# Another order table for the five engine queues of a hybrid decoder layer

## The chip, the cores and the metric

The kernel runs on one core of a Trainium2 chip, in one launch. The metric is the device time of an execution in microseconds (us). The engines are PE (TensorE, matrix products), DVE (VectorE), ACT (ScalarE), POOL (GpSimd) and SP (which here only issues loads). DMA transfers are issued by SP and by POOL.

## What is computed

One decoder layer on x of 512 tokens by 1024 channels, in float32. Two causal mixers run side by side on one input projection, native sparse attention (NSA) and a gated DeltaNet (GDN); a gated feed-forward network (FFN) with a short convolution follows.

```python
h = x @ w_in[l]
...
y_a = nsa_attention(nsa_q, cmp_k, cmp_v, slc_k, slc_v, win_k, win_v, nsa_gate, ...) @ w_nsa_out[l]
y_b = gated_deltanet(gdn_qkv, gdn_beta, gdn_decay, gdn_gate, ...) @ w_gdn_out[l]
mix = (jax.nn.sigmoid(gate_a) * y_a + jax.nn.sigmoid(gate_b) * y_b) @ w_o[l]
x = layer_norm(DEEPNORM_ALPHA * x + mix, ln1_g[l], ln1_b[l])
f = conv_ffn(x, ffn_w_up[l], ffn_conv_w[l], ffn_w_down[l])
x = layer_norm(DEEPNORM_ALPHA * x + f, ln2_g[l], ln2_b[l])
...
def conv_ffn(x, w_up, conv_w, w_down):
    h = causal_dwconv(x @ w_up, conv_w)
    gate, val = jnp.split(h, 2, axis=-1)
    return (jax.nn.silu(gate) * val) @ w_down
```

## The kernel before

Every float32 product is made of three products of rounded parts: a weight block `raw` is loaded (SP), ACT writes its high part `wh` (L481, L1504, L1562), DVE or POOL the rest `wl = raw - wh` (L485, L1505, L1563), and PE multiplies high by high, low by high and high by low. The activations exist as such pairs too (`xh`, `xl`; `mh`, `ml`).

**Stages by time.** Up to about 360 us the kernel does the input projection (`gps`, L495 to L498), the GDN chunks and the NSA heads, interleaved. To 400 us follows the merge, then the output projection and the first norm; from some 480 us FFN-up, from about 705 us FFN-down, at the end the second norm.

**Attention.** For each head and block PE makes scores (`aps`), DVE finds the row minimum (L1072), ACT takes exponentials (L1074), and L1085 scales the probabilities `sc` by the reciprocal sum and the gate, on DVE for most blocks and on POOL for some. PE then transposes `sc` (L1101). The GDN part around it keeps POOL busy: L551 is a power for a norm (`rn0`, `rn1`, `so`) over sums `ss` (L704, from ACT's L703), L485 a `wl`, L746 and L747 masks times decays (`grh`, `grl`), L769 a mask on `at`, L754 a product `db`.

**FFN-up.** 22 groups p of 128 gate and 128 value channels. An ordinary group (`plain`) makes `pu0` (gate) and `pu1` (value) by L1568. Seven groups (`seven`) are made by seven half-size products instead of eight, by L1515, in the PSUM tiles `px`, `pz`, from a combination of weight blocks and of activations (`sh0` to `sh3`, `sl0` to `sl3`, made in `x_sums`); ACT and DVE put the results together in `wf0` and `wf1` (L1524, L1529, L1534, L1537, L1539). A product into `px` cannot begin until the partial sum in it has been copied to `wf`. The combined weights `usum` are built in device memory by POOL's accumulating DMAs; those for FFN-down are `wsum` (L539), those of the output projection `osum`. Each group then passes three taps of the convolution (`fa0`, `fa1`: ACT L1545, twice DVE L1548), a gate `fth` (ACT L1606, DVE L1607, POOL L1608) and is written out as parts for FFN-down (`ph`, `pl`, `sr0` to `sr3`: L1612 to L1623, tiles `pha`, `pla`, `sr0a` and so on).

**Order.** The program is written stage by stage, and a table `QUEUES` then sets the order of every engine's instructions: for each engine the list of its instructions' numbers in the program, in the order in which they are to be issued. `queues` (L348) walks through it and makes every instruction follow the one before it in the list. Each engine works its list strictly in order; an instruction that waits holds up all behind it on that engine. Dependences between engines (data, and buffers to become free) are semaphores, and do not depend on the table. Buffers go round in small sets (`raw`, `wh`, `wl` three each, `raw7` one), so that a load for a later group is issued when the last reader of an earlier one is done.

Of the kernel before, what the change touches and what calls it, by code (L numbers as in the profile page):

```python
# [70 lines left out]
def layout(a):  # L71
# [67 lines left out]
    "PE": """0-9 11-12 10 13-32 41 38 35-37 33 42-43 53 39 34 54 44-45 47-48 40 50-51 46 52 49 56 59 62 57 55 58 65-66 60 63-64 61  # L139
74 68 67 77 71 78 72-73 75-76 86 79 69 87-89 83 70 80 84 81 98 82 99 92-93 85 107 90 108-109 94 110 91 95 111-112 96  # L140
100 113 97 114-115 101-102 116-123 103 124-148 155-178 104 149-151 105 152-153 106 154 183-204 207 205 208 206 209-229
179-182 235 230 236-251 259 252 260 253 261-264 254 265 255 266-267 231-232 256-257 302-303 258 268 233 269-270 304
234 305-307 271-282 308 310-311 360 309 283-298 361-363 312 364-367 313 368 314 369-371 388 315 372 389-390 373-376
391-392 377 393 378 394 379-382 395 383 299-300 396-399 444-445 301 446-450 400-401 416 402-406 417 407-411 418-433
456 434-439 457-459 451 316-317 320 318 321-323 319 460-463 324-327 464-466 328 332-339 329-331 467-472 513 340-347
473-475 348-355 452 476-477 501 356-359 384-387 478-479 514-519 412-415 502-503 520-521 504 522-525 440 453 441 454
442 455 443 526-531 723-725 532 480-484 505 507-508 726-729 533 730 506 485 731 534-536 486-487 509-510 541 732 542
488-489 733-734 490 751-752 735-736 491-492 543 753 737 754-755 493 544 511 494 512 738 495 546-547 739 496 545 497
740 756-757 548 498-499 549 758-760 500 550-551 761 560-561 762 741 763-764 742-744 562 565 552 745 566 746 563-564
537 591 765 592 766 538-540 567 767 581-582 768 553-554 593 568 594-597 569 555 570 598-600 556-557 583 558 585 584  # L150
# [12 lines left out]
1222-1223 1216 1121 1224 924-931 1122 1217 932-935 1225 1123 1233-1234 1124-1125 960 1126-1128 961 1129-1130 962-963
1131-1133 1218 1134-1136 964 1226 965 1235-1236 1227-1228 966 1141-1143 1238 1144-1145 967-968 1239 1146-1149 969 1237
970 1240 1150-1152 971-972 1153-1154 1252 1179 1241 973 1242 1253 1155 1180 974 1181-1182 975 1243 1254-1256 976
1156-1157 1183-1184 1158 1257 1159 1185 1160-1161 1186 1258 1244 1162 1187 1163-1164 1188-1190 1245 1191-1193 1246
1025-1026 1137-1139 1259 1140 1260-1261 1027 1262 1028 1273 1247 1194 1274 1195 1283 1196-1197 1248-1249 1198-1199
1284 1250 1200 1285 1251 1201 1263 1202 1165 1275 1169 1286-1287 1277 1307 1288 1278 1264 1170 1308-1310 1289-1290
1311 1166 1279 1167 1171 1280 1172-1173 1168 1174 1276 1403-1404 1312-1317 1175 1405 1176-1178 1265 1281 1406 1282
1407 1318 1266-1267 1319 1408 1320 1268 1291 1269 1409 1292 1270-1272 1321-1327 1229 1328-1329 1293-1294 1231 1410  # L170
1422-1423 1330 1295 1230 1296 1411 1424-1425 1412 1426 1413 1427 1297-1299 1232 1300-1303 1414 1428 1304 1379 1305
1415 1380 1416-1417 1306 1418 1429-1432 1443-1444 1381-1386 1419-1421 1387-1389 1433-1434 1445 1447-1448 1435 1390
1436 1391 1437 1331 1449 1332 1446 1453 1438-1439 1450-1452 1440 1454 1392 1477 1393-1394 1441 1395-1397 1455 1458
1478 1459 1479 1442 1480 1398 1460 1456-1457 1461-1462 1333 1463 1399 1481 1400-1401 1482-1483 1472-1473 1484-1485
# [1592 lines left out]
```

## Time and profile before

| | us |
|---|---|
| median of 3 runs | 837.82 (837.53 to 840.38) |
| profiled execution | 837.5 |
| its span in the trace | 835.7 |
| PE busy | 806.7 |
| DVE busy | 641.3 |
| ACT busy | 432.1 |
| POOL busy | 195.2 |

The profiled execution lies 0.3 us under the median, and 1.8 us of it lie around the span. Its mean granted clock on TensorE is 0.992. In a group's row of the profile stand line, engine, operation, tiles and shapes; "<-" in brackets names what ended the idle time ahead of it. Line numbers are those of the kernel before. In the new kernel the table is one text line shorter, so that line numbers behind it are one lower there (L1085 becomes L1084).

### The profile page before, as it was taken

To read this page: it belongs to the slowest core of one execution; us is meant where nothing else is said; L and a number is where in the kernel's file an instruction comes from. 1 tells how busy PE (TensorE), PEld (TensorE's weight loads), DVE (VectorE), ACT (ScalarE), POOL (GpSimd) and SP (SyncE) were. 2 spreads that over 40 slices of the span, in tenths; PEclk is the share of its full clock that TensorE was granted. 3 is DMA by queue.
4 is the path that set the end of the run, shared out by engine and by line. 5 is a ranking of instruction groups with operands and counts; after the bars stand their busy time and mean duration, and the time that the engine had idled before them with its cause. 6 is when DMAs were issued, how large, how long until landed. Compare 5 with 4: busy or idle time off the path is not lost.

```text
span 835.7 us, 12479 instructions
## 1 busy us (share of the span) xinstructions
PE 806.7 (97%) x4390; PEld 681.9 (82%) x4390; DVE 641.3 (77%) x1391; ACT 432.1 (52%) x965; POOL 195.2 (23%) x186
## 2 busy tenths in 40 slices
PE   9999999999999999999899999989999999999996
PEld 8788888778788888888787898968788888888875
DVE  5668689889678965565479879857777887788788
ACT  4463686774576764332344235543645654565541
POOL 0334825042275211332100112220011121100001
PEclk9999999999999999999999999999999999999999
DMA  8326129078246936446566697789483468475674
GB/s 277 95 86 214 30 76 249 26 192 186 56 131 156 187 90 153 151 127 153 213 252 203 239 185 234 182 220 201 137 276 114 140 156 197 138 206 173 205 238 148
DMA packets 53406, 139.80 MB, mean 167 GB/s; under 512 B 3936, under 2 KB 5088, under 8 KB 53088
## 3 DMA queue, kind: packets, MB, share of 16 engines
q1 hardware_dynamic: 36064, 92.88, 34.8%
q0 software_dynamic: 17280, 46.14, 24.2%
q8 instruction: 34, 0.56, 0.3%
q14 instruction: 28, 0.23, 0.1%
HBM read 136.91 MB, written 48.23 MB: 222 GB/s over the span
## 4 chain that ended last, share of the span: by engine, by line
PE 77%; DVE 10%; DMA 7%; ACT 3%; issue 2%; POOL 0%; SPq 0%; DVEq 0%; ACTq 0%; POOLq 0%
PE pu L1568 15%; PE gps L495 8%; PE gps L497 8%; PE gps L498 8%; PE px L1645 4%; PE px L1515 4%; PE pz L1645 4%; PE pz L1515 3%; DMA raw<-in_up 2%; PE pout L1115 2%; PE aps L1101 2%; DMA raw<-usum 2%; PE pu L1645 2%; PE pm L495 2%; PE pm L497 2%
## 5 line engine op out<-in xcount | busy, mean ns | idle before, releaser
L495 PE MATMUL gps<-xh,wh 128*128 128x512 f32 x320 | 125.2, 402 | 3.1 <-ACT mt L1147 2.3
L498 PE MATMUL gps<-xh,wl 128*128 128x512 f32 x320 | 125.7, 400 | 0.0
L497 PE MATMUL gps<-xl,wh 128*128 128x512 f32 x320 | 125.1, 399 | 0.0
L1568 PE MATMUL pu<-mh,wh 128*128 128x512 f32 x208 | 80.4, 398 | 2.2 <-ACT wh L1562 2.2
L1568 PE MATMUL pu<-mh,wl 128*128 128x512 f32 x208 | 79.7, 399 | 1.0 <-DVE wl L1563 1.0
L1568 PE MATMUL pu<-ml,wh 128*128 128x512 f32 x208 | 79.8, 396 | 0.0
L1608 POOL TENSOR_TENSOR fth<-fth,fa 128x512 f32<-128x512 f32 x22 | 32.4, 1474 | 197.3 <-DVE fth L1607 150.6
L495 PEld LDWEIGHTS gps<-xh,wh 128*128 128x128 f32 x320 | 60.5, 190 | 15.1 <-issue 3.3
L485 DVE TENSOR_TENSOR wl<-raw,wh 128x512 fp32r<-128x512 f32 x66 | 48.4, 738 | 29.7 <-PE gps L498 13.6
L498 PEld LDWEIGHTS gps<-xh,wl 128*128 128x128 f32 x320 | 60.5, 190 | 11.5 <-POOL wl L485 0.6
L497 PEld LDWEIGHTS gps<-xl,wh 128*128 128x128 f32 x320 | 60.5, 190 | 10.4
L1470 ACT ACTIVATE wh<-raw 128x512 fp32r<-128x512 f32 x67 | 39.9, 626 | 38.9 <-PE px L1645 9.5
L1562 ACT ACTIVATE wh<-raw 128x512 fp32r<-128x512 f32 x52 | 32.6, 628 | 51.5 <-PE pu L1568 41.5
L1471 DVE TENSOR_TENSOR wl<-raw,wh 128x512 fp32r<-128x512 f32 x67 | 44.4, 691 | 16.7 <-ACT wh L1470 16.6
L1563 DVE TENSOR_TENSOR wl<-raw,wh 128x512 fp32r<-128x512 f32 x52 | 38.2, 739 | 21.3 <-ACT wh L1562 18.1
L1504 ACT ACTIVATE wh<-raw 128x512 fp32r<-128x512 f32 x49 | 30.6, 628 | 40.2 <-PE px L1515 15.2
L1548 DVE SCALAR_TENSOR_TENSOR fa<-pu,fcw,fa 128x511 f32<-128x511 f32 (+1 forms) x60 | 44.3, 745 | 7.7 <-ACT fa L1545 7.4
L481 ACT ACTIVATE wh<-raw 128x512 fp32r<-128x512 f32 x46 | 28.8, 627 | 38.4 <-PE gps L497 29.6
L1568 PEld LDWEIGHTS pu<-mh,wh 128*128 128x128 f32 x208 | 39.7, 191 | 8.8 <-ACT wh L1562 2.6
L1568 PEld LDWEIGHTS pu<-mh,wl 128*128 128x128 f32 x208 | 39.6, 191 | 8.8 <-DVE wl L1563 2.6
L485 POOL TENSOR_TENSOR wl<-raw,wh 128x512 fp32r<-128x512 f32 x30 | 41.8, 1413 | 19.9 <-PE gps L498 5.4
L1568 PEld LDWEIGHTS pu<-ml,wh 128*128 128x128 f32 x208 | 39.6, 190 | 6.2
(498 smaller groups left out, 2252.8 us busy)
## 6 DMA issues: line engine op xcount, KB each, us to landing
raw<-in_wT SPq DMA_DIRECT2D x40, 512.0 KB, 3.7
raw<-in_up SPq DMA_DIRECT2D x37, 512.0 KB, 4.6
wsum<-in_down POOLq DMA_DIRECT2D x6, 2816.0 KB, 21.7
usum<-in_up POOLq DMA_DIRECT2D x6, 1792.0 KB, 15.8
raw<-wsum SPq DMA_DIRECT2D x20, 512.0 KB, 3.6
raw<-in_down SPq DMA_DIRECT2D x15, 512.0 KB, 4.3
osum<-in_wo POOLq DMA_DIRECT2D x6, 1024.0 KB, 10.8
wsum<-wsum POOLq DMA_DIRECT2D x2, 2816.0 KB, 15.0
```

The lines of the kernel that those rows point to most:

```text
L485: eng.tensor_tensor(wl, r, wh.bitcast(F32), op=OP.subtract)
L495: i = PE.matmul(ps, wh[k], mh_(k), start=(k == 0), stop=False)
L497: PE.matmul(ps, wh[k], ml_(k), start=False, stop=False)
L498: PE.matmul(ps, wl[k], mh_(k), start=False, stop=(k == n - 1))
L1470: A.activation(hi, raw[:, i], AF.Copy)
L1471: V.tensor_tensor(lo, raw[:, i], hi.bitcast(F32), op=OP.subtract)
L1515: stop=k == 3 and w is lo) if False else PE.matmul(
L1548: V.scalar_tensor_tensor(acc[:, n:], ps[:, :S - n], w[:, i:i + 1], acc[:, n:], op0=OP.mult, op1=OP.add)
L1562: A.activation(hi, r, AF.Copy)
L1563: V.tensor_tensor(lo, r, hi.bitcast(F32), op=OP.subtract)
L1568: q = PE.matmul(ps, w[:, j], x[:, k, :], start=k == 0 and i == 0, stop=k == KD - 1 and i == 2, skip_group_check=True)
L1645: m = PE.matmul(ps, a[x](j)[:, ts], w[y], start=first and i == 0, stop=last and i == 2, skip_group_check=True)
```

## The change

Only the numbers in `QUEUES` change. Every instruction, its engine and its buffers stay as they are; each of the five engines gets them in another order, of which long stretches are the old one (between 180 and 361 us of the profile nothing moves).

```diff
-    "Pool": """2 1 0 8 10 9 12 3 11 13 4 15 5-7 16-17 19 113 20-22 27-28 14 33 25 23 34 29 39 30-32 18 43 40 44 24 41 115 26 54 45 35
-55-36 105 48 42 38 62 37 112 49 51 47 52 64-66 68 107 67 69 57 46 58 50 116 104 92 56 117 59 61 53 63 86 80 87 108 60
...
+    "Pool": """2 1 0 8-9 3 10-13 4 15 5-7 16-17 19 18 20-22 27 14 28 33 25 23 34 29 39 30 105 31-32 40 43 38 37 44 24 41 112 54 35 45
+55 48 36 113 42 49 51 47 52 26 115 107 64-69 50 46 57 62 58 116 104 92 56 117 59 61 53 63 86 80 87 108 60 75 90 76-78
```

Three places show it, in the rows of the queues (line, operation, tiles with their numbers, shape).

**First place, near 168 to 175 us of the profile.** POOL, before and then after (`at`, `grh`, `grl`, `xs` belong to the GDN chunks; `rn0_1930` needs `ss_1929`):

```order
L485 TENSOR_TENSOR wl_2420<-raw_2416,wh_2418 128x512
L485 TENSOR_TENSOR wl_2424<-raw_2416,wh_2422 128x512
L746 TENSOR_TENSOR grh_2134<-cst_321,gdh_340 128x512
L769 TENSOR_TENSOR at_1559<-at_1559,cst_321 128x512
L747 TENSOR_TENSOR grl_2135<-cst_321,gdl_341 128x512
L551 TENSOR_TENSOR rn0_1930<-ss_1929,minus_half_333 128x4
```

```order
L484 TENSOR_TENSOR wl_2420<-raw_2416,wh_2418 128x512
L482 CAST wh_2422<-raw_2416 128x512
L484 TENSOR_TENSOR wl_2424<-raw_2416,wh_2422 128x512
L550 TENSOR_TENSOR rn0_1930<-ss_1929,minus_half_333 128x4
L768 TENSOR_TENSOR at_1559<-at_1559,cst_321 128x512
L745 TENSOR_TENSOR grh_2134<-cst_321,gdh_340 128x512
L793 COPY xs_2188<-cst_321 128x64
L746 TENSOR_TENSOR grl_2135<-cst_321,gdl_341 128x512
```

DVE at the same place, before and then after:

```order
L1105 TENSOR_TENSOR ptl_347<-aps_2270,pth_346 128x2x128
L1076 RECIPROCAL mn_2277<-mn_2277 128x1
L1085 TENSOR_SCALAR sc_2276<-sc_2276,mn_2277,gsig_110 128x384
L1072 ISA sc_2670,mn_2671<-aps_2669,cst_321 128x512
L1072 ISA mn_2671 128x1
L485 TENSOR_TENSOR wl_2529<-raw_2525,wh_2527 128x512
L887 COPY state_2016<-dps_2014 128x128
L1076 RECIPROCAL mn_2671<-mn_2671 128x1
L1072 ISA sc_2685,mn_2686<-aps_2684,cst_321 128x384
L1072 ISA mn_2686 128x1
L704 TENSOR_SCALAR ss_1929<-ss_1929 128x4
```

```order
L1071 ISA sc_2670,mn_2671<-aps_2669,cst_321 128x512
L1071 ISA mn_2671 128x1
L1075 RECIPROCAL mn_2277<-mn_2277 128x1
L1104 TENSOR_TENSOR ptl_347<-aps_2270,pth_346 128x2x128
L703 TENSOR_SCALAR ss_1929<-ss_1929 128x4
L1084 TENSOR_SCALAR sc_2276<-sc_2276,mn_2277,gsig_110 128x384
L886 COPY state_2016<-dps_2014 128x128
```

On POOL `rn0_1930` moved ahead of four operations; on DVE `ss_1929`, which it needs, moved ahead of `sc_2276`, and so did the L1072 pass over `sc_2670`.

The same kind of move stands near 123 us: on DVE `sc_1460` (L1085) came from behind two L1072 passes over `sc_1475` to ahead of them, on POOL `rn1_1088` moved from ahead of `wl_2078` to 14 places later, and on PE the first transpose of `sc_1460` (L1101) moved four products forward.

**Second place, near 541 to 546 us.** DVE in FFN-up, before and then after (`fa0_5903` is the gate half of a `seven` group, `wl_6005` and `wl_6024` are weights of the next):

```order
L1607 SCALAR_TENSOR_TENSOR fth_5860<-fth_5860,fa0_5744 128x512
L1620 TENSOR_TENSOR pla_5440<-fth_5675,pha_5439 128x2x256
L1548 SCALAR_TENSOR_TENSOR fa1_5856<-pu1_5748,fcw_324,fa1_5856 128x511
L1505 TENSOR_TENSOR wl_6005<-raw_6002,wh_6004 128x512
L1548 SCALAR_TENSOR_TENSOR fa0_5903<-wf0_5706,fcw_324,fa0_5903 128x511
L1622 TENSOR_TENSOR sr1a_5442<-sr0a_5441,fth_5590 128x256
L1548 SCALAR_TENSOR_TENSOR fa0_5903<-wf0_5706,fcw_324,fa0_5903 128x510
L1563 TENSOR_TENSOR wl_6024<-raw_6021,wh_6023 128x512
```

```order
L1547 SCALAR_TENSOR_TENSOR fa1_5856<-pu1_5748,fcw_324,fa1_5856 128x511
L1547 SCALAR_TENSOR_TENSOR fa0_5903<-wf0_5706,fcw_324,fa0_5903 128x511
L1547 SCALAR_TENSOR_TENSOR fa0_5903<-wf0_5706,fcw_324,fa0_5903 128x510
L1504 TENSOR_TENSOR wl_6005<-raw_6002,wh_6004 128x512
L1562 TENSOR_TENSOR wl_6024<-raw_6021,wh_6023 128x512
L1606 SCALAR_TENSOR_TENSOR fth_5860<-fth_5860,fa0_5744 128x512
L1504 TENSOR_TENSOR wl_6040<-raw_6002,wh_6039 128x512
```

PE at the same place, before and then after (`px1_5939` can go on only when its sum is copied to `wf0_5942` by ACT; that buffer holds `wf0_5706` until both taps of `fa0_5903` have read it):

```order
L1568 MATMUL pu0_5920<-mh_4006,wl_5964 128x512
L1515 MATMUL pz0_5940<-mh_4006,wl_5986 128x256
L1515 MATMUL px1_5939<-sh1_5456,wh_6004 128x256
L1515 MATMUL px1_5939<-sl1_5457,wh_6004 128x256
L1515 MATMUL px1_5939<-sh1_5456,wl_6005 128x256
L1568 MATMUL pu1_5984<-mh_4006,wh_6023 128x512
L1568 MATMUL pu1_5984<-ml_4007,wh_6023 128x512
```

```order
L1567 MATMUL pu0_5920<-mh_4006,wl_5964 128x512
L1514 MATMUL pz0_5940<-mh_4006,wh_5985 128x256
L1514 MATMUL pz0_5940<-ml_4007,wh_5985 128x256
L1514 MATMUL pz0_5940<-mh_4006,wl_5986 128x256
L1567 MATMUL pu1_5984<-mh_4006,wh_6023 128x512
L1567 MATMUL pu1_5984<-ml_4007,wh_6023 128x512
L1567 MATMUL pu1_5984<-mh_4006,wl_6024 128x512
L1514 MATMUL px1_5939<-sh1_5456,wh_6004 128x256
```

The two taps of `fa0_5903` now stand next to each other and ahead of `wl_6005`, `fth_5860` and `sr1a`; on PE three `pz0` and three `pu1` products come ahead of the first `px1` of the row. On ACT `wf0_5942` still follows `wh_6023`, with two other operations gone from between `wh_6004` and `wh_6023`.

**Third place, near 609 to 636 us.** POOL, before and then after (the DMA copies one combined weight to another in device memory, 2816 KB):

```order
L1608 TENSOR_TENSOR fth_6383<-fth_6383,fa1_6379 128x512
L539 DMA wsum3_103<-wsum2_102 1408x512
L1608 TENSOR_TENSOR fth_6568<-fth_6568,fa1_6564 128x512
L1608 TENSOR_TENSOR fth_6619<-fth_6619,fa1_6615 128x512
L1608 TENSOR_TENSOR fth_6804<-fth_6804,fa1_6800 128x512
```

```order
L1607 TENSOR_TENSOR fth_6383<-fth_6383,fa1_6379 128x512
L1607 TENSOR_TENSOR fth_6619<-fth_6619,fa1_6615 128x512
L538 DMA wsum3_103<-wsum2_102 1408x512
L1607 TENSOR_TENSOR fth_6568<-fth_6568,fa1_6564 128x512
L1607 TENSOR_TENSOR fth_6804<-fth_6804,fa1_6800 128x512
```

The DMA changed places with `fth_6619`, and `fth_6568` went behind it.

Elsewhere: near 585 us, on DVE, `wf1_6179` (L1534) came from behind `wl_6359` (L1505) to ahead of it; near 494 us, on POOL, `fth_5470` came ahead of the two operations of `x_sums`; on POOL the requests of `usum` and `osum` between 65 and 143 us changed places; on SP some neighbouring loads did, and the load of the second norm's rows goes earlier.

More of the change, by code (lines that the diff above doesn't have):

```diff
@@ new lines @@
+1686 1680 1694 1687 1657 1681 1688-1689 1706 1695 1690 1696 1707-1708 1697 1691 1709-1710 1692-1693 1711-1714
+1698-1700 1715-1720 1701-1702 1721-1722 1730-1731 1723 1732 1724 1703-1705 1725 1733-1734 1726-1728 1735 1729 1736
+1742 1737-1738 1743 1754 1739 1755 1744-1745 1756-1757 1740-1741 1746 1758 1747 1759-1760 1748 1761 1749 1762
+1750-1751 1763-1767 1752 1768-1769 1778 1770-1771 1779 1772-1774 1780 1753 1781-1782 1775 1783 1776 1784-1786 1777
+1787-1788 1802 1789-1792 1803 1814-1815 1804 1816 1793-1794 1817 1795 1805 1796 1806 1818-1819 1807 1797 1808-1813
@@ new lines @@
+2002-2004 2018 2005 2019 2006 2020-2022 2030 2023 2031 2024-2027 2007 2032 2008 2028 2033-2034 2029 2009-2010 2035
+2011 2036-2038 2012-2013 2039-2040 2014 2041-2043 2015 2054-2055 2044-2046 2056 2047-2048 2057-2058 2049 2059
+2016-2017 2060-2063 2050-2051 2066-2068 2064 2069 2052 2065 2053 2070-2071 2075 2072-2074 2078 2076-2077 2093
+2081-2082 2094-2095 2090 2083 2091 2114 2087 2117 2088-2089 2115-2116 2092 2099 2096 2120 2079 2100 2097 2080 2101
+2084 2098 2105 2121 2085 2118-2119 2123 2122 2106 2086 2126 2141 2102 2127-2128 2124-2125 2107 2132 2103-2104 2142
@@ new lines @@
+4105-4106 4079-4080 4107-4109 4081-4082 4110 4083-4094 4111 4095-4098 4112-4131""",
+    "DVE": """0 27 104 1-4 6 5 7 9 8 10-11 13 12 14-17 58 18 59-60 19 61 23 21 64-65 22 66 20 26 62 31 90 32 67 63 33 72 34 30 35-36
+24 37 73 38-52 74 53-54 68-71 83 29 84 55 81 92 82 93 91 85-86 115 56 87 94 88 95 75 80 25 151 153 76 152 154 77 109
+107 164 102 108 110-111 79 112-114 96-97 166 98 165 116 99 89 117-118 28 119-121 100 122-123 101 285 103 124-126 167
+155 127-129 156-157 130-132 158 133 212 134-136 57 137-141 168-169 142-144 173 145 170 174-175 146-147 105 172 176 106
@@ new lines @@
+1300-1301 1296-1297 1302 1304 1275 1303 1285 1299 1298 1306 1305 1291 1308 1307 1287 1309-1310 1277 1281 1311-1315
+1317 1316 1318-1323 1325 1324 1326""",
+    "Activation": """0-6 8 7 9-10 31 12 11 14 13 16 15 20 26 17 27 21 23 33 24 18-19 22 28 25 34-35 29-30 41 36 42-45 37-40 46 61 51-52 62
+53-55 67 47-49 68 56 32 50 82 63 57 64 58-59 83 60 65-66 69-73 84 74 85 75 110 93 111 76-77 94 103 125 104 78 105 112
+126 113 86 121 120 150 123 122 79-81 114 87-89 115 151 90-92 95-97 127 98-102 141 140 106 116-118 107-108 128 109 124
@@ L345 @@
+145-146 144 147-155 157-172 156 173-186 188 190 192 194-201 187 202 191 193 203 189 204-205""",
 }
```

387 lines of the change are left out of this document (182 added, 205 removed).

## The prediction

> **What bounds the kernel now.** I read the page first: busy shares, then the chain that ended last.
>
> ```profile
> span 835.7 us, 12479 instructions
> PE   806.7 (97%) x4390; PEld 681.9 (82%) x4390; DVE 641.3 (77%) x1391; ACT 432.1 (52%) x965; POOL 195.2 (23%) x186
> PE 77%; DVE 10%; DMA 7%; ACT 3%; issue 2%; POOL 0%; SPq 0%; DVEq 0%; ACTq 0%; POOLq 0%
> ```
>
> TensorE (PE) is busy for 806.7 of 835.7 us, and its instructions don't change. An order can return only the 29.0 us in which PE stands still, and time in which its clock is low. The list of waits says for whom it stands still (last number: the longest one), and the table by stretches of time says where and at which clock (the number behind POOL's is the granted clock, the next the DMA share).
>
> ```profile
> PE aps L1101 <- DVE sc L1085: 3.0, 2, 1.7
> PE gps L495 <- ACT mt L1147: 2.3, 1, 2.3
> PE pu L1568 <- ACT wh L1562: 2.2, 2, 1.2
> PE px L1515 <- ACT wf L1524: 1.8, 1, 1.8
> PE px L1515 <- ACT wh L1504: 1.2, 1, 1.2
> ...
> 120.00:180.00 60.00, 55.48 (x352) 45.73 (x351) 55.99 (x177) 43.48 (x124) 27.02 (x31) 1.00 0.54 132
> 530.00:570.00 40.00, 36.26 (x204) 31.19 (x203) 25.93 (x46) 17.95 (x34) 8.72 (x6) 0.91 0.94 215
> 530.00:640.00 110.00, 100.81 (x596) 87.83 (x595) 78.29 (x137) 54.38 (x103) 17.71 (x13) 0.97 0.76 199
> 640.00:720.00 80.00, 79.78 (x426) 68.36 (x425) 65.95 (x107) 40.53 (x74) 12.81 (x9) 1.00 0.56 151
> ```
>
> So the waits are few and long, in the attention stage's end (120 to 180 us, PE idle 4.5) and in FFN-up (530 to 640, idle 9.2). I take them one by one.
>
> **The change, part by part.** No instruction is removed or added; each engine gets another order. From 180 to 361 us it is the old one, and I count nothing there.
>
> *The two waits for L1085.* The first rows give that line's shortest, median and longest; then follows the second wait.
>
> ```profile
> L1085 DVE TENSOR_SCALAR sc<-sc,mn,gsig x26: 327/475/5099, 106.0 to 285.2; 128x512 f32<-128x512 f32 x9, 128x128 f32<-128x128 f32 x8, 128x384 f32<-128x384 f32 x5, 128x256 f32<-128x256 f32 x4
> 123.65 2.58 DVE L1085 TENSOR_SCALAR sc<-sc,mn,gsig 128x512 f32<-128x512 f32 x1
> 126.28 0.33 PE L1101 MATMUL aps<-ident,sc 128*128 128x128 f32 x1 [1.33 <-DVE sc L1085]
> ...
> 168.34 3.05 POOL L485 TENSOR_TENSOR wl<-raw,wh 128x512 fp32r<-128x512 f32 x2
> 169.74 5.10 DVE L1085 TENSOR_SCALAR sc<-sc,mn,gsig 128x384 f32<-128x384 f32 x1
> 172.04 0.20 ACT L703 ACTIVATION_READ_ACCUMULATOR junk<-dps 128x1 f32 x1
> 173.08 1.53 POOL L747 TENSOR_TENSOR grl<-cst,gdl 128x512 fp32r<-128x512 f32 x1
> 174.90 0.55 PE L1101 MATMUL aps<-ident,sc 128*128 128x128 f32 x3 [1.66 <-DVE sc L1085]
> ```
>
> An operation whose median is 0.475 us took 5.10, from 169.74 to 174.84, as long as GpSimd (POOL) ran five operations without a gap (168.34 to 174.61, the first pair and the last quoted). It ended when they did. In the new order DVE first does ss_1929, and POOL, after its two L485, waits for that same result (rn0_1930 now stands before grh, at, grl). POOL therefore has a gap just when sc_2276 is due. ss_1929 waits for ACT's last L703 pass (172.04 + 0.20), so sc_2276 should start around 172.4 and be done near 172.9; PE is free at 174.90 - 1.66 = 173.24. The wait of 1.66 goes. At 126.28 sc_1460 stands two places earlier, ahead of both L1072 passes over sc_1475, a POOL operation (rn1_1088) has left its way, and PE asks for it four matmuls earlier: even from its old start it would end at 123.65 + 0.5 = 124.2, and it starts earlier by the two passes; PE needs it at 126.28 - 1.33 less the four matmuls, about 124. That takes away 1.33. If POOL still runs under either, the whole 3.0 stays.
>
> The Trainium skill, "SBUF — State Buffer", section "Who interferes with whom", has the two engines lock each other out for one whole instruction. By that rule the DVE operation would have gone ahead after POOL's current instruction; the row of 5.10 us disagrees, and shows a hold over five. By the rule no 1.66 would be there to gain, and the sum below would be that much less.
>
> *The wait at 545.97 and the slow clock behind it.* PE waits for wf0 (L1524, ACT), which waits for two DVE taps (L1548).
>
> ```profile
> 541.16 0.69 DVE L1607 SCALAR_TENSOR_TENSOR fth<-fth,fa 128x512 f32<-128x512 f32 x1
> 543.10 0.68 DVE L1505 TENSOR_TENSOR wl<-raw,wh 128x512 fp32r<-128x512 f32 x1
> 544.37 0.42 DVE L1622 TENSOR_TENSOR sr1a<-sr0a,fth 128x256 f32<-128x256 f32 x1
> 545.53 0.38 ACT L1524 ACTIVATE wf<-px 128x256 f32<-128x256 f32 x1 [1.03 <-DVE fa L1548]
> 545.97 0.39 PE L1515 MATMUL px<-sh,wh 128*128 128x256 f32 x1 [1.79 <-ACT wf L1524]
> ...
> 543.04:546.45 3.41, 1.62 (x10) 1.18 (x10) 3.41 (x8) 1.52 (x3) 0.00 (x0) 1.00 1.12 238
> 546.45:549.86 3.41, 3.41 (x15) 3.02 (x14) 2.01 (x4) 0.63 (x1) 0.00 (x0) 0.50 1.10 255
> 563.52:566.93 3.41, 3.17 (x8) 2.51 (x9) 2.72 (x7) 0.59 (x2) 0.00 (x0) 0.50 1.08 201
> 621.55:624.96 3.41, 1.60 (x9) 1.19 (x7) 0.43 (x2) 0.72 (x2) 0.00 (x0) 1.00 1.01 266
> 624.96:628.37 3.41, 3.17 (x21) 2.92 (x22) 2.04 (x4) 1.31 (x3) 1.29 (x1) 1.00 0.26 103
> ```
>
> The first three DVE rows quoted (0.69 + 0.68 + 0.42 = 1.8) now stand behind the taps: wf0 is no longer last. PE also gets three pz and three pu1 products ahead of px1 (about 1.0 us of its own work). What is late next is wh_6023 and wl_6024, for pu1: about 0.4 of idle is left, so 1.4 of 1.79 goes. Behind the wait stands a stretch at clock 0.50: 3.41 us that do 1.7 us of work at full clock. It begins where 1.62 of the preceding 3.41 us were busy. With 0.4 idle the preceding stretch is nearly full, so I count these 1.7 too. Bounds: 0, since 1.60 busy at 621.55 was not followed by 0.50 but by 1.00 (the two last rows); 1.7 at most. I take the upper end, since the preceding stretch would be far fuller than either. The stretch at 0.50 from 563.52 stays.
>
> "TensorE: Matmul & The Clock Gate" in the Trainium skill, section "HAM oscillation — how this bites in real kernels", sets the limit at idle gaps of over about 3.4 us. The trace disagrees: no wait of this kernel is over 2.3, and one of 1.79 is followed by clock 0.50. By that rule the 1.7 would not return with the wait, and the sum below would be 1.7 less.
>
> *The wait at 562 to 564* (L1562 and L1563) keeps its chain through DVE, POOL's L1608 and ACT: 0, between -0.3 and +0.5 (ACT operations of 0.6 change places in it).
>
> *The waits at 579.22, 586.78, 589.85 and 625.20.*
>
> ```profile
> 571.07 7.44 DMA raw<-usum
> 586.78 0.36 PE L1515 MATMUL px<-mh,wh 128*128 128x256 f32 x1 [0.92 <-DVE wf L1534]
> 610.49 0.92 POOL L539 DMA_DIRECT2D wsum<-wsum  x1
> 616.39 7.75 DMA raw<-usum
> 625.20 0.39 PE L1515 MATMUL px<-sh,wh 128*128 128x256 f32 x1 [2.04 <-ACT wf L1529]
> 631.07 4.64 DMA raw<-in_up
> 634.71 1.29 POOL L1608 TENSOR_TENSOR fth<-fth,fa 128x512 f32<-128x512 f32 x1 [6.74 <-DVE fth L1607]
> 641.26 0.33 SPq L1497 DMA_DIRECT2D raw<-usum  x1
> 646.04 0.62 ACT L1504 ACTIVATE wh<-raw 128x512 fp32r<-128x512 f32 x1
> wsum<-wsum POOLq DMA_DIRECT2D x2, 2816.0 KB, 15.0
> ```
>
> At 579.22 a load ends the wait, and its issue stays tied to the same DVE operation: 0. At 586.78 wf1 (L1534) now stands ahead of the L1505 it followed; that L1505 is next late, some 0.2, so 0.7 goes. At 589.85 ACT's two candidates swap: 0. At 625.20 the load took 7.75 us, in flight with POOL's wsum copy issued at 610.49 (15.0 in flight, to 625.5). The copy now stands behind fth_6619, which ran at 634.71. The nearest load without it took 4.64: this one would land at 616.39 + 4.64 = 621.0, its two ACT operations (0.62 and 0.38 in the rows) end by 622.1, and PE is busy until 625.20 - 2.04 = 623.16. So 2.0 goes. The copy is then in flight from somewhere between 631 and 635 for 15.0, to 646 or 650, where the loads issued from 641.26 on are wanted from 646.04 on: some slack, priced as a rival.
>
> *What moves without a wait there*: fth_5470 ahead of x_sums on POOL, usum and osum requests shifted on POOL, a few loads exchanged on SP, ph/pl/sr writes put off on DVE. Their cover is PE's work: in 640 to 720 it is busy for 79.78 of 80. If the cover is gone, each costs one wait of the known sizes (0.9 to 2.3).
>
> Sum: 1.33 + 1.66 + 1.4 + 1.7 + 0.7 + 2.0 = 8.8. Against it I set 2.4 for new waits, two of 1.2 (L1504's, the middle of the list), between 0 and all of 8.8; the order changes over some 640 us, so none at all is unlikely. The profiled execution took 837.5: 837.5 - 8.8 + 2.4 = 831.1. The median of the runs is 837.82, 0.3 above it: 831.4.
>
> **The rivals.**
> 1. *The time is given back.* FFN-up is near its transfers: the DMA share is 0.94 from 530 to 570, and the load at 571.07 took 7.44. A PE that arrives 3 us earlier would wait for the next load. Then only L1085's 3.0 and the 2.0 at 625.20 count, less the 2.4: 837.8 - 2.6 = 835.2. For it: the chain passes through loads at 571.07, 616.39 and 631.07. Against it: each load is issued by a buffer coming free, which moves forward with PE.
> 2. *The holds stay*, because POOL and DVE are both released by ss_1929 and POOL starts first: 3.0 less, 834.4; PE would show the same two waits on L1085.
> 3. *Slower: the wsum copy in its new place.* If loads from 641.26 on take 7.75, the first lands at 649.0 against 646.04 (3.0 late), and the two load rounds behind it (at 646 and 653) are also about 3 late: 9.0, and with it two stretches at 0.50, 3.4. The gains stand and are outweighed: 831.4 + 9.0 + 3.4 = 843.8. It decides from a copy that lasts beyond 655, 24 us instead of 15.0. Against it: the second load round comes when a copy of 15.0 is over.
>
> 4. *The slow stretch is not set by the wait before it*, and comes at another place: 831.4 + 1.7 = 833.1, still faster. The row of 1.60 busy without a slow stretch behind it speaks for it, the one of 1.62 with one against. This is also what the page on the clock gate would give.
>
> **How the numbers follow.** My forecast has 0.52, the fourth rival 0.10, given back 0.16, holds stay 0.10, slower by the copy (or another such chain) 0.12. A measurement here can tell about 0.5% (4.2 us) from no change. The forecast and the fourth rival lie below 833.6: faster 0.62. The next two lie within: 0.26. Slower 0.12. Range: nothing given back and the slow stretch behind 562 gone too would be 837.8 - 8.8 - 1.7 = 827.3, so 827 below; above, 839.5 takes in both middle rivals with one more slow stretch (835.2 + 1.7 = 836.9) and a first step of the third (3.0), and leaves out most of that one. The forecast's own range is 827 to 834.
>
> **What would show it.** In the profile after: no PE wait on L1085 above 0.3, and its longest duration far below 5.1; no stretch at 0.50 around 543; the load for the group at 616 back to under 5.5 us, and PE's wait on L1529 gone; the waits on L1147 (2.3), and near 562 and 579, still there. PE busy in 640 to 720 below 79 of 80 would speak for the third rival. I am wrong if PE's idle time is as before but in other places.

## The result, and the profile after

The changed kernel takes 827.67 us (median of 4 runs, 826.3 to 828.94); the kernel before took 837.67 beside it (4 runs, 837.01 to 840.38). The ratio is 0.988, with a 95% interval of 0.986 to 0.990: 10.0 us less, where 6.4 were forecast. In the changed kernel's profile the line numbers are one lower; in the kernels of the experiments they are those of before.

The head of the page, then the list of waits (total, number, longest):

```profile
span 826.0 us, 12475 instructions
PE 803.1 (97%) x4390; PEld 680.1 (82%) x4390; DVE 630.6 (76%) x1391; ACT 432.1 (52%) x965; POOL 192.7 (23%) x186
```

```profile
PE pu L1567 <- ACT wh L1561: 3.5, 2, 2.5
PE gps L494 <- ACT mt L1146: 2.3, 1, 2.3
PE pu L1567 <- DVE wl L1562: 1.7, 2, 1.1
...
PE pz L1514 <- DVE wf L1536: 1.0, 1, 1.0
```

PE stands still for 826.0 - 803.1 = 22.9 us instead of 29.0: 6.1 less. Its busy time, with the same products, is 3.6 less; together that is the 9.7 us of the span. One stretch at half clock fewer (below) accounts for 1.7 of the 3.6 (3.41 us at clock 0.50 do half the work). The rest I cannot place; the ends of PE's records are modelled. The waits on L1085 (now L1084), on `wf` at L1524, L1529 and L1534, and on L1504 are gone from the list; those on L1561 and L1562 (before: L1562, L1563) have grown, and the one on L1536 is new. The table by stretches of time says where the idle time went:

```profile
120.00:180.00 60.00, 58.79 (x375) 49.72 (x374) 52.13 (x186) 45.52 (x129) 27.89 (x31) 1.00 0.66 166
530.00:570.00 40.00, 35.38 (x201) 30.08 (x200) 28.13 (x46) 19.03 (x36) 4.61 (x4) 0.96 1.02 227
530.00:640.00 110.00, 103.69 (x617) 90.77 (x616) 83.97 (x141) 57.78 (x108) 13.54 (x11) 0.97 0.73 198
```

From 120 to 180 us the idle time fell from 4.52 to 1.21, so by 3.3. From 530 to 640 it fell from 9.19 to 6.31, by 2.9. Together that is 6.2, about the whole 6.1. In 530 to 570, however, PE is idle for 4.62, more than before (3.74).

**The place near 170 us.** The group's row (shortest, median, longest), then DVE and POOL of the changed kernel:

```profile
L1084 DVE TENSOR_SCALAR sc<-sc,mn,gsig x26: 331/474/844, 105.1 to 281.2; 128x512 f32<-128x512 f32 x9, 128x128 f32<-128x128 f32 x8, 128x384 f32<-128x384 f32 x5, 128x256 f32<-128x256 f32 x4
169.73 0.17 DVE L703 TENSOR_SCALAR ss<-ss 128x4 f32<-128x4 f32 x1
169.81 0.47 DVE L1084 TENSOR_SCALAR sc<-sc,mn,gsig 128x384 f32<-128x384 f32 x1
...
169.98 1.20 POOL L550 TENSOR_TENSOR rn<-ss,minus_half 128x4 f32<-128x4 f32 x1 [1.88 <-DVE ss L703]
```

The longest L1084 on DVE is 0.844 us, where 5.10 stood. POOL stands still for 1.88 us waiting for `ss`, and `sc` starts in that gap.

**The place near 545 us, and what is late next.** First some windows of 3.41 us (the first one holds the `wf0` of the old wait, which ACT now writes at 537.03), then the largest of PE's stalls from 536 to 600 us and what the longest hangs on (ACT, DVE, POOL); the last row is from the kernel before.

```profile
534.45:537.86 3.41, 3.41 (x24) 3.03 (x22) 2.91 (x5) 1.67 (x4) 0.00 (x0) 1.00 1.13 211
551.52:554.93 3.41, 0.73 (x2) 0.30 (x2) 1.71 (x2) 2.15 (x5) 2.90 (x2) 1.00 0.34 64
554.93:558.34 3.41, 3.31 (x8) 2.63 (x9) 3.11 (x7) 1.82 (x4) 0.00 (x0) 0.50 1.09 180
578.83:582.24 3.41, 1.73 (x9) 1.04 (x8) 2.89 (x4) 2.11 (x5) 1.56 (x2) 1.00 0.49 194
582.24:585.65 3.41, 3.41 (x11) 2.72 (x10) 3.37 (x7) 1.76 (x3) 0.00 (x0) 0.50 0.00 0
```

```profile
553.24 0.50 PE L1567 MATMUL pu<-mh,wh 128*128 128x512 f32 x1 [2.53 <-ACT wh L1561]
555.03 0.79 PE L1567 MATMUL pu<-mh,wl 128*128 128x512 f32 x1 [1.05 <-DVE wl L1562]
...
580.34 0.50 PE L1567 MATMUL pu<-mh,wh 128*128 128x512 f32 x1 [0.99 <-ACT wh L1561]
...
548.66 0.63 ACT L1605 ACTIVATE fth<-fa 128x512 f32<-128x512 f32 x1 [1.65 <-DVE sr1a L1621]
551.47 0.63 ACT L1618 ACTIVATE pha<-fth 128x512 fp32r<-128x512 f32 x1 [2.17 <-POOL fth L1607]
...
552.57 0.62 ACT L1561 ACTIVATE wh<-raw 128x512 fp32r<-128x512 f32 x1
553.22 1.75 DVE L1562 TENSOR_TENSOR wl<-raw,wh 128x512 fp32r<-128x512 f32 x1 [3.20 <-ACT wh L1561]
552.28 2.13 POOL L1607 TENSOR_TENSOR fth<-fth,fa 128x512 f32<-128x512 f32 x1
...
560.18 0.63 ACT L1619 ACTIVATE pha<-fth 128x512 fp32r<-128x512 f32 x1 [3.02 <-POOL fth L1608]
```

Where `wf0` made PE wait, PE is now busy for the whole 3.41 us. But the weights of the next group come late: on ACT `wh` (552.57) stands behind a `pha` that waits 2.17 us for POOL's `fth`. It stood behind the same `pha` in the kernel before (560.18, `wh` at 561.56), where PE waited 1.17 us for it. Now PE is 10.4 us earlier here and this `wh` only 9.0, so the wait is 2.53. The chain that leads to it (`fth` on ACT, DVE and POOL, then `pha`) is held at its start, where ACT waits 1.65 us for DVE's `sr1a`, one of the operations that the new order put off. The `wl` behind it takes 1.75 us beside the next `fth` (1.49 before; the same operation at 555.99, with POOL idle, takes 0.69). Behind this wait, and behind the one at 580, clock 0.50 follows.

**The place near 610 to 625 us.** The load for the group whose wait was at 625.20 (third column: median from issue to landing), and POOL:

```profile
raw<-usum SPq DMA_DIRECT2D x1, 256.0 KB, 2.8
```

```profile
609.00:624.00 15.00, 15.00 (x99) 13.60 (x98) 12.40 (x22) 7.80 (x15) 3.03 (x3) 1.00 0.44 133
...
620.96 1.30 POOL L1607 TENSOR_TENSOR fth<-fth,fa 128x512 f32<-128x512 f32 x1 [18.42 <-DVE fth L1606]
622.21 0.92 POOL L538 DMA_DIRECT2D wsum<-wsum  x1
```

The load took 2.8 us in place of 7.75 (the copy is not yet in flight), and PE is busy for 15.00 of 15.00. `fth_6619` itself runs at 620.96, 13.75 earlier than before (634.71), so that the copy behind it is issued at 622.21 and not after 634.

### The profile page after: what moved, and what is told of

Read it like the earlier page. It is cut to its first block, busy times and chain, and to the rows that moved or that the text cites. A ratio compares the mean times of both kernels' runs of the same rounds, so it can differ in the third digit from the quotient of the medians.

```text
span 826.0 us, 12475 instructions
## 1 busy us (share of the span) xinstructions
PE 803.1 (97%) x4390; PEld 680.1 (82%) x4390; DVE 630.6 (76%) x1391; ACT 432.1 (52%) x965; POOL 192.7 (23%) x186
## 5 line engine op out<-in xcount | busy, mean ns | idle before, releaser
L497 PE MATMUL gps<-xh,wl 128*128 128x512 f32 x320 | 123.6, 397 | 0.0
L496 PE MATMUL gps<-xl,wh 128*128 128x512 f32 x320 | 123.4, 395 | 0.0
L1562 DVE TENSOR_TENSOR wl<-raw,wh 128x512 fp32r<-128x512 f32 x52 | 39.1, 754 | 22.2 <-ACT wh L1561 12.3
L1561 ACT ACTIVATE wh<-raw 128x512 fp32r<-128x512 f32 x52 | 32.7, 629 | 40.5 <-PE pu L1567 34.2
L1567 PEld LDWEIGHTS pu<-mh,wh 128*128 128x128 f32 x208 | 39.8, 192 | 10.1 <-ACT wh L1561 3.9
```

The source lines that it names most:

```text
L496: PE.matmul(ps, wh[k], ml_(k), start=False, stop=False)
L497: PE.matmul(ps, wl[k], mh_(k), start=False, stop=(k == n - 1))
L1561: A.activation(hi, r, AF.Copy)
L1562: V.tensor_tensor(lo, r, hi.bitcast(F32), op=OP.subtract)
L1567: q = PE.matmul(ps, w[:, j], x[:, k, :], start=k == 0 and i == 0, stop=k == KD - 1 and i == 2, skip_group_check=True)
```

## The experiments

All times are medians; "before" was run beside each group: 837.58, then 838.07, then 837.39. To see where each kernel gains, I matched its PE instructions with those of the kernel before and took the median difference of their start times, over the 10 to 15 us from the time named (time in the kernel before, us; negative is earlier). Where PE's own order changes it is good to about 1 us.

| time before | after | early_only | late_only | gap_only | copy_only | taps_only |
|---|---|---|---|---|---|---|
| 110 | +0.2 | +0.2 | +0.2 | -0.4 | 0.0 | +0.6 |
| 150 | -1.7 | -1.7 | +0.2 | -0.4 | 0.0 | +0.6 |
| 180 | -4.0 | -4.1 | +0.2 | -1.6 | 0.0 | +0.6 |
| 410 | -5.3 | -3.9 | +0.4 | -2.5 | 0.0 | -0.4 |
| 530 | -6.8 | -4.5 | -1.1 | -2.7 | +0.1 | -0.3 |
| 550 | -10.1 | -4.6 | -4.5 | -2.7 | +0.1 | -1.4 |
| 590 | -7.1 | -6.3 | -1.4 | -2.7 | 0.0 | -1.2 |
| 630 | -9.4 | -5.0 | -3.5 | -3.1 | -2.3 | +0.5 |
| 670 | -10.7 | -4.7 | -5.0 | -3.1 | +0.7 | +0.6 |
| 810 | -10.0 | -5.3 | -5.5 | -4.4 | +0.3 | +0.2 |

**early_only and late_only** split the table in the stretch where it doesn't change: one has the new order up to there and the old one behind, the other the reverse.

```diff
-"PE": before[:1000] + before[1000:]     "DVE" cut at 500, ACT 300, POOL 100, SP 50
+"PE": after[:1000]  + before[1000:]     early_only
+"PE": before[:1000] + after[1000:]      late_only
```

> The new order up to 178 us alone, the old one behind it. If the gain is a sum of separate places, this is worth what PE's instructions between 180 and 360 us come earlier in the trace of the new order, 4.0 us: 837.7 - 4.0 = 833.7, with one slow-clock stretch (1.7) more or less by where its windows fall. In the trace no PE wait on L1085 over 0.3. Rival, the later stages are bound by their transfers and take it back: 837 or more.

Measured: 832.78, ratio 0.994 (0.992 to 0.997), so 4.8 less.

> The old order up to 178 us, the new one behind it. If the places are separate, the rest of the 10.0: 837.7 - 6.0 = 831.7, and the two waits on L1085 (3.0 us) stay. Rival, the places hang together and the later part needs the earlier one: 835 or more.

Measured: 832.41, ratio 0.993 (0.991 to 0.995), so 5.2 less. The two sum to 10.0, the whole effect. Each has an interval of about 2 us either way; within that the halves neither need nor hurt each other. An earlier PE did not just wait for the next load in FFN-up: early_only keeps its lead from 180 to 670 (-4.1, then -4.7).

**gap_only** takes one place alone into the kernel before.

```diff
 POOL
+L551 rn0_1930
 L746 grh_2134
 L769 at_1559
 L747 grl_2135
-L551 rn0_1930
 DVE
+L704 ss_1929
 L1085 sc_2276
 ...
-L704 ss_1929
```

> The old order with two rows moved: on POOL rn0_1930 ahead of grh, at and grl, on DVE ss_1929 to just ahead of sc_2276. Theory, the DVE operation is held by GpSimd operations that run without a gap, and a gap frees it: L1085's longest falls from 5.1 us to 2.6 (the other held one), the PE wait of 1.66 at 174.90 goes, 837.7 - 1.7 = 836.0. Rival, the lock is for one instruction and something else kept PE waiting: L1085 short or not, the wait stays and the time is 837.7.

Measured: 835.74, ratio 0.998 (0.995 to 1.000); PE is 1.2 earlier behind the place (-0.4 to -1.6 in the table). The step from -1.6 to -2.5 at 410 comes with a stretch at half clock that this execution does not have there.

**gap_undone** is the reverse in the changed kernel: `rn0_1930` goes back behind `grl`, nothing else.

```diff
 POOL
-L551 rn0_1930
 L769 at_1559
 L746 grh_2134
 L794 xs_2188
 L747 grl_2135
+L551 rn0_1930
```

> The changed kernel with one row moved: on GpSimd rn0_1930 stands again behind at, grh and grl, as in the kernel before, so that GpSimd runs its operations around 170 us without a gap for ss_1929. Everything else is the changed order. Theory (the VectorE operation sc_2276 is held for the whole uninterrupted run of GpSimd operations): its duration goes back from 0.47 us to 3 to 5 us, TensorE waits again for L1085 at about 171 to 173 us, and TensorE is 1.2 to 1.7 us later from there on; the time rises by that, to about 829, and by nothing else but a shift of half-clock stretches (1.7 each, either sign). Rival (the gain there came from the order on VectorE, where the row maximum of sc_2670 went ahead): duration below 1 us, TensorE at most 0.5 later.

Measured: 828.22, ratio to before 0.988 (0.983 to 0.994), and PE against the changed kernel unmoved at this place (+0.3 at 160 and at 180 us). These are the rival's numbers; its reason, the order on DVE, is not shown by them. POOL now runs without a gap, and `sc` is still not held (DVE, then POOL):

```profile
170.00 0.63 DVE L704 TENSOR_SCALAR ss<-ss 128x4 f32<-128x4 f32 x1
170.54 0.47 DVE L1085 TENSOR_SCALAR sc<-sc,mn,gsig 128x384 f32<-128x384 f32 x1
...
169.56 1.04 POOL L746 TENSOR_TENSOR grh<-cst,gdh 128x512 fp32r<-128x512 f32 x1
170.55 0.23 POOL L794 COPY xs<-cst 128x64 f32<-128x64 f32 x1
170.75 1.17 POOL L747 TENSOR_TENSOR grl<-cst,gdl 128x512 fp32r<-128x512 f32 x1
```

So my theory of the hold did not cover this case. Three kernels, timed once each, look into it.

**ss_only** moves only the DVE row of gap_only, **rn_only** only its POOL row, both in the kernel before; **xs_behind** is gap_undone with the short copy `xs_2188` moved behind `rn0_1930` as well.

```diff
 DVE, ss_only                    POOL, rn_only
+L704 ss_1929                   +L551 rn0_1930
 L1085 sc_2276                   L746 grh_2134
 ...                             ...
-L704 ss_1929                   -L551 rn0_1930
```

> The kernel before with one row moved: on VectorE ss_1929 (L704) stands just ahead of sc_2276; GpSimd keeps its order and runs L485 twice, grh, at, grl and then rn0_1930, without a gap. Read by the duration of sc_2276 near 170 to 175 us and by TensorE's wait on it. Theory as predicted (a VectorE operation of this kind is held as long as GpSimd runs on without a gap): sc_2276 starts behind ss_1929 near 172.4 and ends only with grl near 174.6, duration 2 us, TensorE's wait stays at 1.4 to 1.7. Rival (what counts is the moment at which the operation is issued; it gets in at the next boundary between two GpSimd operations): duration 0.5 to 1.4 us, done by 173.7, TensorE's wait at most 0.5.

> The kernel before with one row moved: on GpSimd rn0_1930 ahead of grh, at and grl; VectorE keeps its order, so that rn0_1930 waits for ss_1929, which stands behind sc_2276. GpSimd therefore stands still behind its two L485, from about 171.4 us. Both theories let sc_2276 end near 171.9 (duration about 2.2, held by the second L485 only), and TensorE, free at 173.24, does not wait. If the duration is still over 3 us, the hold does not come from GpSimd's operations at all. What was put off on GpSimd (grh, at, grl, about 4 us later) may make another wait: 0 to 1.

> The changed kernel with rn0_1930 and also the short copy xs_2188 (128x64) moved behind grl, so that GpSimd runs L485, wh, L485, at, grh, grl in a row and the short copy is no longer between them, at the moment at which sc_2276 is due (170.5 us with rn0_1930 alone moved back, where it took 0.47). Theory (the short copy between two long operations is what let it in): sc_2276 takes 1.3 to 2.5 us, TensorE waits 0.3 to 1.2 for it. Rival (it gets in at whichever boundary comes next): 0.47 again, at the boundary between grh and grl, and TensorE waits no more than 0.3.

Measured once each: 832.75, 838.57 and 828.59. One time says little (the kernel before alone ran from 833.15 to 842.39 beside the experiments), so the records have to tell. The rows of ss_only (DVE, POOL, PE), of rn_only (DVE, and a line of its waits) and of xs_behind (DVE, POOL):

```profile
172.12 2.38 DVE L704 TENSOR_SCALAR ss<-ss 128x4 f32<-128x4 f32 x1 [2.57 <-ACT junk L703]
174.42 0.47 DVE L1085 TENSOR_SCALAR sc<-sc,mn,gsig 128x384 f32<-128x384 f32 x1
170.68 1.56 POOL L746 TENSOR_TENSOR grh<-cst,gdh 128x512 fp32r<-128x512 f32 x1
171.69 1.78 POOL L769 TENSOR_TENSOR at<-at,cst 128x512 f32<-128x512 f32 x1
172.94 1.53 POOL L747 TENSOR_TENSOR grl<-cst,gdl 128x512 fp32r<-128x512 f32 x1
174.94 0.55 PE L1101 MATMUL aps<-ident,sc 128*128 128x128 f32 x3 [1.84 <-DVE sc L1085]
```

```profile
169.87 1.87 DVE L1085 TENSOR_SCALAR sc<-sc,mn,gsig 128x384 f32<-128x384 f32 x1
PE dps L890 <- POOL at L769: 3.9, 1, 3.9
```

```profile
170.96 1.28 DVE L1085 TENSOR_SCALAR sc<-sc,mn,gsig 128x384 f32<-128x384 f32 x1
170.98 1.04 POOL L747 TENSOR_TENSOR grl<-cst,gdl 128x512 fp32r<-128x512 f32 x1
```

In ss_only the hold is only passed on: `ss`, an operation of 0.17 us, takes 2.38, until `grl` is over, and PE waits no less than before (1.84, then 1.66). In rn_only the hold ends when POOL stops (1.87 us), PE no longer waits for `sc`, but `at` comes some 4 us later and PE waits 3.9 for it, where I had expected 1 at most. Each row alone is worth nothing or less; only both bring the 1.2. In xs_behind, without the short copy, `sc` is held for one operation (`grl`) and PE waits 0.52.

What tells the long holds from the short ones is in POOL's records. In ss_only each begins well before the one ahead has ended (171.69 against 170.68 + 1.56 = 172.24), as in the kernel before, where five overlapped by about 0.5; in gap_undone and xs_behind they overlap by 0.03 to 0.05. In the traces, every L704, L1085 and L483 on DVE that took over 0.25 us longer than the shortest of its shape waited out one POOL operation at most, unless POOL's records overlapped by over 0.5; then it waited for the first operation whose successor did not overlap it, or for POOL to stop. That is a regularity of the records, not shown as a cause: no run here forced an overlap, and longer records on POOL may as well be an effect of the hold (`grl` took 1.53 in ss_only, 1.04 in xs_behind).

**copy_only** makes the POOL exchange alone in the kernel before, **copy_undone** takes it back in the changed kernel.

```diff
 POOL, copy_only                 POOL, copy_undone
 L1608 fth_6383                  L1608 fth_6383
-L539 DMA wsum3                 +L539 DMA wsum3
 L1608 fth_6568                  L1608 fth_6619
 L1608 fth_6619                 -L539 DMA wsum3
+L539 DMA wsum3                  L1608 fth_6568
```

> The old order with one row moved: POOL's copy into wsum3 behind fth_6619. Theory, the copy in flight made the load at 616 us take 7.75 us: that load falls under 5.5, the PE wait of 2.04 at 625.20 goes, 837.7 - 2.0 = 835.7. Rival, the loads from 641 us on now run into the copy and PE waits there: 837.7 or more, with a new wait at L1515 near 645 to 660.

Measured: 837.09, ratio 0.999 (0.997 to 1.001): nothing. The wait of 2.04 goes (-2.3 at 630), and 3.0 come back by 670. The copy is issued at 633.65 there, and the load that then flies with it takes 7.44 (2.6 before); PE waits for its `wh` (chain, then waits):

```profile
639.03 7.44 DMA raw<-usum
PE px L1515 <- ACT wh L1504: 2.9, 2, 1.9
```

> The changed kernel with the wsum copy moved back ahead of fth_6619 (order on GpSimd fth_6383, copy, fth_6619, fth_6568). Theory (the copy's place sets the length of the load that flies with it): the load near 615 us takes over 7 us again, TensorE waits some 2.0 us for L1529 near 620 us, and the end is 2.0 later, 829.7, since nothing behind has slack to return it. Rival A (the rest of the late order already gives slack there, the load comes early enough): no wait, the end is the same within 0.5. Rival B (the copy then ends early, and later loads gain what this one loses, as with the copy moved alone in the kernel before): 2.0 later at 625, but back by 660.

Measured: 830.89, ratio to before 0.992 (0.989 to 0.995), 3.2 above the changed kernel, and PE 3.1 later at 620 with nothing given back (chain, then PE):

```profile
611.30 6.98 DMA raw<-usum
619.34 0.39 PE L1515 MATMUL px<-sh,wh 128*128 128x256 f32 x1 [2.76 <-ACT wf L1529]
```

So the same exchange is worth 0 in the old order and about 3 in the new one. With the copy issued at 633.65 PE waits for the load of 639.03; with the copy at 622.21 it waits for none from 582 to 660 us. That load does not escape the copy in the changed kernel:

```profile
629.89 0.33 SPq L1496 DMA_DIRECT2D raw<-usum  x1
```

Issued here, it takes 6.7 us with the copy in flight and lands at 636.57, just before ACT makes its `wh` (636.68) without waiting for it. So `fth_6619`, on which the copy's moment hangs, is only part of the reason; what else gives this load its room in the new order no run separates.

**taps_only** makes the change near 541 to 546 us alone in the kernel before.

```diff
 DVE
 L1548 fa1_5856
+L1548 fa0_5903 (twice)
 L1505 wl_6005
 L1563 wl_6024
+L1607 fth_5860, L1620 pla, L1622 sr1a
 ACT
+L1524 wf0_5942 ahead of L1619 pha, L1545 fa1_5907
 PE
+L1515 pz0_5940 x3, L1568 pu1_5984 x3
 L1515 px1_5939
```

> The kernel before with the one place near 541 to 546 us changed: on VectorE the two taps of fa0_5903 ahead of wl_6005, fth_5860, pla and sr1a, on TensorE three pz0 and three pu1 products ahead of the first px1, on ScalarE the operations that the taps do not need put behind wf0_5942. Theory as predicted: the wait of 1.79 at 545.97 falls to about 0.4 (TensorE 1.4 earlier from there), and the half-clock stretch from 546.45 goes too (another 1.7); if nothing gives it back, 837.6 - 3.1 = 834.5. Rival A (given back): what was put off, fth_5860 and the weights behind it, is late at the next places, 553 to 566, and TensorE is 0 to 0.5 earlier by 570. Rival B (the half-clock stretch does not hang on the wait): TensorE 1.4 earlier and another stretch of 3.41 us at half clock within the next 20 us.

Measured: 836.75, ratio 0.999 (0.996 to 1.002). The wait for `wf0` and the slow stretch at 546 go, but three microseconds later PE waits as long for a weight that DVE has not made:

```profile
549.24 0.39 PE L1515 MATMUL pz<-sh,wl 128*128 128x256 f32 x1 [1.74 <-DVE wl L1505]
```

PE is some 1.0 earlier from 550 to 620, and this is gone by 630: another stretch at 0.50 comes behind 624. So the wait moved on, as rival A says, though more than its 0.5 was left at 570, and a slow stretch took the rest, as in rival B but later. In time, the gain is not clear of the noise.

**ahead** starts from the changed kernel and puts the writers of the next weights ahead of gate and convolution operations, at 553 and at 580 us; **ahead2** adds two more such moves, for the waits that ahead showed.

```diff
 ACT, ahead (the first of the two places)
 L1504 wh_6122
+L1562 wh_6159
 L1606 fth_5911
+L1504 wh_6182, L1539 wf0_5942, L1562 wh_6199
+L1504 wh_6221                  (ahead2)
 L1619 pha_5439
 L1545 fa0_5980
-L1562 wh_6159 ...
```

> The changed kernel with the ScalarE and VectorE writers of the next group's weights (wh_6159, wh_6182, wf0_5942, wh_6199, wl_6160, and the same for 6395 to 6436) put ahead of the gate and convolution operations that they followed, at the two places where the changed kernel shows new waits, near 553 to 555 us (2.53 for wh, 1.05 for wl) and 580 to 582 us (1.0 and 0.7). Theory (the weights are late because they stand behind operations that nobody waits for): these waits, 5.3 us together, go; with one half-clock stretch less behind them up to 7; something of it returns in later places as in the changed kernel itself, so about 823 to 824. Rival (the loads themselves, or the put-off operations, set the pace in FFN-up): the waits move by one group and the time stays within 1.5 of the changed kernel.

Measured: 828.95, ratio to before 0.989 (0.985 to 0.994): no better than the changed kernel, which is its rival's outcome. The waits have moved to the next weights in the same queue (waits, ACT):

```profile
PE pz L1515 <- ACT wh L1504: 5.3, 2, 3.0
557.88 0.42 ACT L1612 ACTIVATE pha<-fth 128x256 fp32r<-128x256 f32 x1 [1.62 <-POOL fth L1608]
```

> The kernel with the weights' writers put ahead, with two more moves for the two waits that it showed in place of the removed ones (pz waits 2.99 us at 559.44 and 2.34 at 586.88 for L1504, which stands behind gate and convolution operations on ScalarE): wh_6221 goes ahead of pha, and wh_6457 ahead of fa0_6216, on ScalarE, wl_6222 and wl_6458 forward with them on VectorE. Theory (each of these waits is one more writer in the wrong place): both go, 5.3 us, and with them the half-clock stretch at 588, another 1.7; part comes back as before, so 824 to 826, below the changed kernel's 827.7. Rival (FFN-up cannot go faster here, since the convolution's operations, put off, are themselves late): other waits of together 4 to 5 us, and 828 to 830.

Measured: 823.08 (5 runs, 822.89 to 824.93), ratio to before 0.983 (0.980 to 0.987): the fastest kernel of this study, 14.3 below the one before. Its span is 820.7. Its busy shares and one stretch:

```profile
PE 799.5 (97%) x4390; PEld 678.2 (83%) x4390; DVE 633.1 (77%) x1391; ACT 431.9 (53%) x965; POOL 193.1 (24%) x186
...
530.00:640.00 110.00, 104.87 (x642) 92.22 (x641) 89.31 (x145) 60.37 (x114) 15.63 (x12) 1.00 0.72 200
```

Of the 5.3 us that its span lies below the changed kernel's, PE's idle time gives 1.7 (22.9 to 21.2) and its busy time 3.6: the clock is 1.00 throughout FFN-up, with no stretch at 0.50. Here the late weights cost more in clock than in waiting.

## Why the prediction was right, step by step

The time, 827.67, lies inside the range, 3.7 below the forecast and at the lower edge of the forecast's own range. In the profiled execution idle time is 6.1 less, where the terms make 1.33 + 1.66 + 1.4 + 0.7 + 2.0 - 2.4 = 4.7, and busy time 3.6 less, where one slow stretch of 1.7 was counted. Two terms came true for another reason than the one given (at 174.90 and the copy), and which slow stretches would go was not foreseen: that the sum came this near is in part luck.

- *The wait at 126.28 (1.33).* Right in size: PE is 1.5 earlier past it. No run takes this place alone, so which of its three moved rows did it stays open.
- *The wait at 174.90 (1.66).* The size is right (PE gains 1.9 there), the reason half. A gap on POOL does end a hold (rn_only), and both moved rows are needed in the old order (1.2, gap_only). But in the changed kernel `sc` was due at 169.81, not 172.4, and putting POOL's row back costs nothing there (gap_undone). Another 0.6 between the two places was not in the sum.
- *The rule of one instruction.* What the page "SBUF — State Buffer" of the Trainium skill says in its section "Who interferes with whom" fits xs_behind, where `sc` waits out one operation, and not ss_only, 2.38 us over three.
- *The wait at 545.97 and its slow stretch (1.4 + 1.7).* Right as to the place: PE is 3.3 earlier at 550. By itself the change keeps 1.0 to 620 us and nothing at the end (taps_only).
- *"0" at 562 to 564 and 579.22.* Wrong, the first largest. The chain through POOL's `fth` and ACT did stay, with the same `pha` ahead of the `wh`, but the step from there to 0 fails: an unchanged chain leaves the wait unchanged only if it comes forward with PE. PE came 10.4 us earlier and the `wh` 9.0, held behind the put-off `sr1a`. The waits on L1561 and L1562 rose from 2.2 and 1.0 to 3.5 and 1.7, with another 1.0 on L1536: 3.0 given back, against 2.4 allowed. The wait at 579.22, said to stay because a load ends it, is gone.
- *The wait at 586.78 (0.7).* Gone; two of 0.99 and 0.69 near 580 stand in its place, in the 3.0.
- *The copy (2.0).* The wait went, for 3.1 as copy_undone shows. The reason given, the copy's new place, is not enough: the forecast put the copy between 631 and 635, and copy_only, which has it there, gives all of it back through the third rival's chain (a load of 7.44). In the new order the copy comes earlier than that, since `fth_6619` runs 13.75 us earlier, which I had not followed; the load that flies with it takes 6.7 there too, and PE does not wait for it.
- *The slow stretches.* The profiled execution before had three ahead of the kernel's end (from 403.09, 546.45, 563.52), after two (from 554.93 and 582.24). The one counted did go, as did the one at 563.52 that "stays"; others came behind new waits. The one at 403.09 went too, though the wait ahead of it is still 2.28. That one went and others came by where the windows fell (below) was in no term of the sum. The fourth rival was right in that the stretch is not set by the wait alone. The limit of about 3.4 us for an idle gap, in "TensorE: Matmul & The Clock Gate" of the Trainium skill, section "HAM oscillation — how this bites in real kernels", is not where the limit lies here: only rn_only has a wait above it (3.9, and clock 0.50 follows), while in the changed kernel waits of 0.99 and 0.69 within one window are followed by 0.50 too.

What no run separates: about 1 us near 470, which late_only has and early_only has not.

## What to carry to other kernels

Price a moved row by what it needs beside it: of three places tried alone in the old order two showed no gain clear of the noise, and one of these was worth 3 us in the new order. When PE comes earlier, ask of each chain that it waits for whether the chain comes earlier by as much. When a wait on a late weight is removed, look at once for the next weight behind the same convolution operation in the same queue; here two rounds of that were needed before the time fell. Count PE's idle time in each window of 3.41 us: from about 1.7 us, in one wait or in several, a slow stretch can follow.

## What the runs showed of the hardware

**The slow stretches lie on a grid of 3.413 us.** From 403.09 to 546.45 are 42 of these, to 563.52 five more; in the changed kernel eight lie between 554.93 and 582.24. Every stretch at 0.50 in the fourteen traces lies on such a grid. Whether one comes goes with how busy PE was in the window ahead of it, not with how long one wait was. The same wait of 2.28 us (L1147, now L1146) fell into one window before, and across two after:

```profile
399.68:403.09 3.41, 1.13 (x5) 0.84 (x5) 2.91 (x6) 1.68 (x3) 1.85 (x2) 1.00 0.47 126
403.09:406.50 3.41, 3.41 (x9) 2.63 (x9) 2.87 (x8) 2.01 (x5) 0.00 (x0) 0.50 0.97 368
```

```profile
394.50:397.91 3.41, 1.89 (x9) 1.24 (x7) 2.13 (x4) 0.00 (x0) 3.35 (x3) 1.00 0.16 47
397.91:401.33 3.42, 2.66 (x12) 2.22 (x13) 2.79 (x7) 3.40 (x7) 0.00 (x0) 1.00 0.94 321
```

Over all windows of the grid in these traces from 20 us on, those at full clock with up to 1.48 us busy were all followed by 0.50, those with 1.79 and more all by 1.00, and between 1.52 and 1.77 both occurred. Two windows that were themselves at 0.50 (2.38 us busy in xs_behind, 2.75 in gap_undone) were followed by another one. Each stretch costs up to 1.7 us, so an order that moves PE by a microsecond can gain or lose 1.7 far from where it changed. ss_only shows it: PE is where it was until 340 us, its idle time is 27.9 (29.0 before), and its profile has one stretch ahead of the end instead of three; it took 832.75 at a mean granted clock of 0.996. The kernel before itself took 833.15 and 833.48 in its two executions at 0.996, and 841.87 and 842.08 in the two at 0.986.

**A DVE operation can be held over several POOL operations in a row** (5.10, 2.58 and 2.38 us, for operations of 0.47, 0.54 and 0.17).

**A copy of 2816 KB in flight turned a load of 256 KB from 2.6 to 2.8 us into one of 6.7 to 7.75.** copy_only moves nothing but the copy: the load issued at 616.39 falls from 7.75 to 2.8, and the one that met the copy later rises from 2.6 to 7.44.
